# A two-layer hybrid encoder on one core: an eighth up group in seven products, early pairs split by ScalarE and DMA, and the last gate's units in program order

## The chip, the cores and the metric

The kernel runs on one core of a Trainium2 chip. Time is microseconds (us) of device time of one execution. The engines are TensorE (PE), VectorE (DVE), ScalarE (ACT), GpSimd (POOL) and SyncE (SP); SP issues the plain loads, POOL the transfers that add to what stands at their target.

## The reference

Two layers run over x of 512 tokens by 1024 channels, in float32. What matters here is cut out of the reference:

```python
for l in range(DEPTH):                       # DEPTH = 2
    h = _rmsnorm(x, g_mix[l])
    proj = h @ w_in[l]                       # gates of 4 branches, and each branch's own inputs
    ...
    y_a = _conformer_conv(a_in, ...)         # GLU, depthwise conv of width 31, LayerNorm, swish
    ...
    branch = jnp.einsum('bsnc,ncd->bsnd', ys, w_branch[l])
    gates = jax.nn.sigmoid(gate_pre.reshape(bsz, seq, N_BRANCH, D_MODEL) + gate_b[l])
    mixed = jnp.sum(gates * branch, axis=2)
    x = x + mixed @ w_out[l]
    x = x + _conv_ffn(_rmsnorm(x, g_ffn[l]), w_up[l], ffn_conv_w[l], ffn_conv_b[l], w_down[l])

def _conv_ffn(h, w_up, conv_w, conv_b, w_down):
    u = _depthwise_conv(h @ w_up, conv_w, conv_b)          # 1024 -> 2 x 2816, conv width 3
    gate, up = jnp.split(u, 2, axis=-1)
    return (jax.nn.silu(gate) * up) @ w_down
```

## The kernel before

Everything is held with channels on the partitions and the 512 tokens along the row. A float32 operand is split into a high part that TensorE takes in one pass and a low part, the rest; one product is then three matmuls: high by high, high by low, low by high. Both the weights and the activations are split so. A weight unit (128 partitions by 1024) is loaded by SP into `w_raw`; ACT copies it into `w_hi` (L269, or L1277 for units of a seven-product group), and DVE subtracts to make `w_lo` (L271, L1278). `w_raw` has two buffers, `w_hi` and `w_lo` three each, and units are made two ahead.

**Whole units and seven products.** A whole unit multiplies one weight unit by the full 512 tokens, in 24 matmuls of 512 columns (`block`, L290 to L292). Four of them make one group of the up projection (two gate blocks and two up blocks). For some groups, `SEVEN`, the group is instead treated as a 2 by 2 block product and worked out with seven smaller products rather than eight: seven units of 24 matmuls with 256 columns each (`seven`, L1130), named A11, A12, A22, S1, S2, S3 and S4. The activations' sums and differences (`form` tiles) are made once a layer. The weights' sums grow in place: POOL issues a transfer that adds another quarter of the weight matrix to a tile already used (`grow`, L1259, target `chain` or `w_raw`). Copies of partial results (`sv`, L1142, by ACT) and sums (DVE) put the seven products together.

**The last gate.** Each layer's four branches have a gate. The gate of branch `ORDER[3]`, the conv branch, runs last and as two such groups, `ga` and `gb`, 14 units in all (`last_gate`, `gate_unit`, L936). `GATE_STEPS` gives the order of the units in the program. Meanwhile a generator, `conv`, does the conv branch in steps: at each `tick` after half a unit it takes one. It transposes the conv's result (L471), makes the LayerNorm's mean and spread, normalises into `cv` tiles (L487), waits two ticks, and transposes back (L496). After unit 12 and unit 14 four branch products each follow (`branch`), and then the output projection, whose operand is `mh`.

Instructions go to the engines in an order that a scheduler chooses at build time: it takes the program's order as priority and moves an instruction back when what it needs (a PSUM bank, a buffer) is not yet free by its reckoning. Two helpers bend it: `after_mm` ties an instruction behind the last matmul in the order without a wait, and `first()` raises priority.

**The up projection.** `up_steps` makes the list of steps: whole groups 0 and 1, then the seven-product groups, whose units are interleaved with those of the next group, then the rest whole; the first two whole units after them are `held` between the last seven-product units. Each finished block is multiplied by `RB` into `U` (L1216), then goes through the width-3 convolution (`conv_part`, L1171 to L1173), and Silu (`fth`), and the product of gate and up is `f`, two blocks to a tile.

**Pairs and the down projection.** The down projection is a seven-product one too, over 11 pairs of `f` blocks, and needs each pair's sums (`sum`) and the high and low parts of all of them: `split_pair` makes them, with high copies by ACT (L1354) and low subtractions by DVE (L1355). The first six pairs are split during the up projection: after blocks 15 to 20, `EARLY`. The rest are split one at a time in the down projection's loop. `pair_tags` says into which old buffers the parts go.

```python
EARLY = (15, 16, 17, 18, 19, 20)
...
        if i in EARLY:
            self.split_pair(self.F, EARLY.index(i), self.got)
```

Of the kernel before, what the change touches and what calls it, by code (L numbers as in the profile page):

```python
# [3 lines left out]

# [2 lines left out]

# [23 lines left out]

CHUNK = 4

SEVEN = (2, 3, 4, 5, 6, 7)


def up_steps():
# [17 lines left out]
              ('gb', 'A22'), ('ga', 'S2'), ('ga', 'S1'), ('gb', 'S2'), ('gb', 'S1'), ('ga', 'S4'), ('gb', 'S4')]  # L57
MIX = (0, 1, 4, 5, 2, 3, 6, 7)

EARLY = (15, 16, 17, 18, 19, 20)  # L60
EPS = 1e-6
BIG = 1e30
EB = 4
# [167 lines left out]
class Trunk:  # L231
# [214 lines left out]
    def conv(self):  # L446
# [36 lines left out]
        for h in range(2):  # L483
# [3 lines left out]
                v.tensor_scalar(un[:, b * 256:(b + 1) * 256], pss[h][:, b * 256:(b + 1) * 256], mv[:, tb, 0:1],  # L487
                                r[:, tb:tb + 1], ALU.subtract, ALU.mult)
            uns.append(un)
        for _ in range(2):  # L490
            yield
        yh, yl = self.y_tiles()
        for j in range(2):
# [428 lines left out]
    def gate_unit(self, g, n):  # L922

        b = g, {'S3': 'B', 'A22': 'B', 'A12': 'C'}.get(n, 'A')
        start = n in ('S3', 'A11', 'A12')
        if start:
            self.banks[b] = self.mm() if n == 'A12' else self.aux()
        ps = self.banks[b]
        hi, lo = self.unit()
        for e in range(2):  # L930
            o = ps[:, e * 256:(e + 1) * 256]
            for j in range(4):
                s = slice((2 * j + e) * P, (2 * j + e + 1) * P)
                xh, xl = self.gate_x(n, j)
                for i, (w, x) in enumerate(((hi, xh), (hi, xl), (lo, xh))):
                    self.last_mm = self.nc.tensor.matmul(o, lhsT=w[:, s], rhs=x, start=start and not (e or j or i),  # L936
                                                         stop=j == 3 and i == 2, skip_group_check=True)
            self.tick()
        self.gate_done(g, n, ps)

# [222 lines left out]
    def conv_part(self, i, s):  # L1163

        nc = self.nc
        v = nc.vector
        c = i + s * NF
        u = self.U[s][:, i % 2]
        y = self.fp.tile([P, S], F32, name=f"cy{s}", tag=f"cy{s}", bufs=2)
        w = lambda t: self.par('ffn_conv_w', c * 3 + t)  # L1170
        nc.scalar.activation(y, u[:, 1:513], AF.Identity, scale=w(1), bias=self.par('ffn_conv_b', c))  # L1171
        v.scalar_tensor_tensor(y, u[:, 0:512], w(0), y, ALU.mult, ALU.add)
        v.scalar_tensor_tensor(y, u[:, 2:514], w(2), y, ALU.mult, ALU.add)  # L1173

        if s == 0:
            si = self.fp.tile([P, S], F32, name="fth", tag="fth", bufs=2)
            nc.scalar.activation(si, y, AF.Silu)
            self.silus[i] = si
            return
        if self.last and i % 2 == 1 and i // 2 < KT:  # L1180
            self.turn_res(i // 2)
        if i % 2 == 0:
            self.fpair = self.fp.tile([P, 1024], F32, name="f", tag=f"fp{i // 2}", bufs=1)
        fl = self.fpair[:, i % 2 * S:(i % 2 + 1) * S]
        v.tensor_tensor(fl, y, self.silus.pop(i), ALU.mult)
        self.F.append(fl)
        if i in EARLY:
            self.split_pair(self.F, EARLY.index(i), self.got)

    def ffn(self, l, last):  # L1190
        nc = self.nc
# [2 lines left out]
        for i in range(2):  # L1194
# [2 lines left out]
            nc.gpsimd.memset(u[:, :, 513:514], 0.0)  # L1197
            self.U.append(u)
        self.F, self.got, self.silus, self.sevens, self.last = [], {}, {}, {}, last
        self.seven_forms()  # L1200
        held = {}
        self.pace = 0.0
        for kind, a, b in UP_STEPS:
            if kind == 'seven':
                self.seven(a, b)
                continue
            if kind == 'free':
                ps = held.pop((a, b))
            else:
                ps = self.mm()  # L1210
                self.block(ps)
                self.tick()
            if kind == 'held':
                held[a, b] = ps
            else:
                v.tensor_tensor(self.U[b][:, a % 2, 1:513], ps, self.RB, ALU.mult)  # L1216
                self.conv_part(a, b)
        for g in self.slow:
            for _ in g:
# [93 lines left out]
    def pair_tags(self, j):  # L1313

        x = [f"x{n}{d}" for d in range(KT) for n in 'hl']
        late = [(f"lt{n // 2}", n % 2) for n in range(10)]
        hi = [f"fh{2 * j}", f"fh{2 * j + 1}"] if j < len(EARLY) else x[2 * (j - len(EARLY)):][:2]
        lo = ["lo", "lo"] if j == 0 else [(f"fp{j - 1}", 0), (f"fp{j - 1}", 1)]  # L1320
        a = (["e0", "e1"], ["e2", "e3"], ["e4", "e5"], late[0:2], late[2:4], late[4:6],
             ["xr", "xr"], ["xn", "xn"], ["cy0", "cy0"], ["cy1", "cy1"], x[10:12])[j]
        s4 = (late[6:8], late[8:10], ["e6", "e7"], x[12:14], x[14:16], ["t3", "t2"])[j // 2]
        return hi + lo + a + s4

    def conv_tile(self, tag):
# [3 lines left out]
    def split_pair(self, F, j, got):  # L1330
# [2 lines left out]
        v = nc.vector  # L1333
        fi, fk = F[2 * j:2 * j + 2]

        def tile(t):
            if isinstance(t, tuple):
                t, n = t
                if n == 0:
                    self.halves[t] = self.fp.tile([P, 1024], F32R, name=f"p{t}", tag=t, bufs=1)  # L1340
                return self.halves[t][:, n * S:(n + 1) * S]
            pool = self.xpool if t[:2] in ("xh", "xl") else self.fp
            return pool.tile([P, S], F32R, name=f"p{t}", tag=t, bufs=2 if t in ("lo", "xr", "xn", "cy0", "cy1") else 1)
# [353 lines left out]
```

## Time and profile before

| what | value |
|---|---|
| median of three runs | 1544.81 us (1544.36 to 1545.08) |
| the profiled execution | 1543.59 us |
| its span, first to last instruction | 1541.8 us |
| matmuls on PE | 8274 |
| up projection, layer 0 | 439.3 to 664.0 us |
| up projection, layer 1 | 1206.1 to 1433 us |
| last gate, layer 0 / layer 1 | from 333.2 / from 1099.7 us |

The median and the profiled execution are about 1.2 us apart, and the span leaves out what lies before the first and after the last instruction. In a timeline row come the start, the duration (both us), the engine, the line and operation, output and input by the program's names, the shape, a count, and in brackets the idle time before it with what ended it. A matmul's duration is longer than the distance to the next, because matmuls overlap: the pace is read from the starts. `<-DVE w_lo L1278` says that DVE's instruction on line 1278 ended the idle time.

### The profile page before, as it was taken

The page shows a single profiled execution, that of the slowest core. Times are in us where ns is not written, and L with a number is a line of the kernel's source. Part 1 is how long each engine was busy: PE and PEld are TensorE (multiplying, and loading weights), DVE is VectorE, ACT ScalarE, POOL GpSimd, SP SyncE. Part 2 cuts the span into 40 slices and gives each one's busy share as a digit, 9 for nine tenths or more (in the row PEclk, how much of TensorE's full clock was granted, in tenths as well). Part 3 has the DMA queues.
Part 4 walks back from the last instruction along what each step waited for, and adds up shares of the span by engine and source line. Part 5 has one row for each costly group of instructions (what it writes and reads, how often), then busy time and mean ns, then how long its engine had stood idle before and what let it go on. Part 6 is the DMA issues. An engine that isn't in the chain of part 4 may idle for free.

```text
span 1541.8 us, 22905 instructions
## 1 busy us (share of the span) xinstructions
PE 1528.9 (99%) x8274; PEld 1322.0 (86%) x8274; DVE 1308.0 (85%) x2210; ACT 942.8 (61%) x1580; POOL 187.7 (12%) x288
## 2 busy tenths in 40 slices
PE   9999999999999999999999999999999999999999
PEld 8888888889889999888888888888898899988887
DVE  6689988797789999996576899887986899999974
ACT  6677777356456665564548687673564566655643
POOL 0123002321001110000002130023200011100000
PEclk9999999999999999999999999999999999999999
DMA  7789586856656886366568795867566589852674
GB/s 236 227 229 203 164 181 152 181 151 148 208 168 141 178 182 162 96 205 203 180 185 255 203 202 174 171 161 182 146 150 215 171 173 230 182 155 96 191 229 161
DMA packets 117153, 278.58 MB, mean 181 GB/s; under 512 B 27440, under 2 KB 29360, under 8 KB 117040
## 3 DMA queue, kind: packets, MB, share of 16 engines
q1 hardware_dynamic: 87088, 187.98, 38.2%
q0 software_dynamic: 29664, 88.62, 30.5%
q8 instruction: 65, 1.06, 0.3%
q10 hardware_dynamic: 288, 0.52, 0.1%
q14 instruction: 48, 0.39, 0.1%
HBM read 259.25 MB, written 58.72 MB: 206 GB/s over the span
## 4 chain that ended last, share of the span: by engine, by line
PE 85%; DVE 8%; ACT 3%; issue 2%; DMA 2%; POOL 0%; ACTq 0%; DVEq 0%; POOLq 0%
PE mm L291 14%; PE mm L290 14%; PE mm L292 14%; PE aux L1130 11%; PE aux L936 3%; PE aux L1376 3%; PE aux L1378 3%; PE aux L1377 3%; PE mm L520 2%; PE mm L521 2%; PE mm L522 2%; PE mm L1376 2%; PE mm L1378 2%; PE mm L1377 2%; PE mm L1130 2%
## 5 line engine op out<-in xcount | busy, mean ns | idle before, releaser
L269 ACT ACTIVATE w_hi<-w_raw 128x1024 fp32r<-128x1024 f32 (+1 forms) x241 | 251.1, 1043 | 232.5 <-PE mm L291 83.3
L271 DVE TENSOR_TENSOR w_lo<-w_raw,w_hi 128x1024 fp32r<-128x1024 f32 (+1 forms) x241 | 290.5, 1207 | 72.8 <-ACT w_hi L269 71.3
L290 PE MATMUL mm<-xh,w_hi 128*128 128x512 f32 x768 | 300.2, 391 | 0.0
L291 PE MATMUL mm<-xl,w_hi 128*128 128x512 f32 x768 | 299.5, 390 | 0.0
L292 PE MATMUL mm<-xh,w_lo 128*128 128x512 f32 x768 | 299.3, 390 | 0.0
L292 PEld LDWEIGHTS mm<-xh,w_lo 128*128 128x128 f32 x768 | 144.2, 188 | 30.6
L290 PEld LDWEIGHTS mm<-xh,w_hi 128*128 128x128 f32 x768 | 144.3, 188 | 29.0
L291 PEld LDWEIGHTS mm<-xl,w_hi 128*128 128x128 f32 x768 | 144.3, 188 | 28.3
L1130 PE MATMUL aux<-form,w_hi 128*128 128x256 f32 x768 | 140.2, 283 | 1.4 <-ACT sv L1142 1.4
L1130 PEld LDWEIGHTS aux<-form,w_hi 128*128 128x128 f32 x768 | 120.0, 192 | 2.5 <-ACT sv L1142 2.2
L1130 PE MATMUL aux<-form,w_lo 128*128 128x256 f32 x384 | 108.7, 283 | 0.0
L1277 ACT ACTIVATE w_hi<-chain 128x1024 fp32r<-128x1024 f32 x64 | 67.6, 1057 | 53.7 <-DMA chain<-W 11.5
L457 DVE SCALAR_TENSOR_TENSOR cv<-cv,prm 128x512 f32<-128x512 f32 x120 | 94.6, 788 | 0.7
L1278 DVE TENSOR_TENSOR w_lo<-chain,w_hi 128x1024 fp32r<-128x1024 f32 x64 | 77.9, 1219 | 17.0 <-ACT w_hi L1277 16.7
L1171 ACT ACTIVATE cy<-U,prm 128x512 f32<-128x512 f32 x88 | 68.4, 808 | 32.2 <-DVE U L1216 21.0
L520 PE MATMUL mm<-w_hi,xh 128*128 128x512 f32 x192 | 76.4, 398 | 0.3 <-DVE V L648 0.3
L1277 ACT ACTIVATE w_hi<-w_raw 128x1024 fp32r<-128x1024 f32 x48 | 50.6, 1053 | 42.4 <-PE aux L1130 21.1
L521 PE MATMUL mm<-w_lo,xh 128*128 128x512 f32 x192 | 74.9, 390 | 0.0
L522 PE MATMUL mm<-w_hi,xl 128*128 128x512 f32 x192 | 74.8, 390 | 0.0
L1259 POOL DMA_DIRECT2D chain<-W x48 | 42.1, 876 | 260.4 <-DVE w_lo L1278 233.1
L1130 PEld LDWEIGHTS aux<-form,w_lo 128*128 128x128 f32 x384 | 73.7, 192 | 0.0
L777 ACT ACTIVATE e<-e,rl 128x256 f32<-128x256 f32 (+2 forms) x96 | 57.3, 597 | 21.8 <-DVE rl L776 21.5
(376 smaller groups left out, 3837.7 us busy)
## 6 DMA issues: line engine op xcount, KB each, us to landing
w_raw<-W SPq DMA_DIRECT2D x191, 512.0 KB, 4.1
sums<-W POOLq DMA_DIRECT2D x24, 1024.0 KB, 11.5
chain<-W POOLq DMA_DIRECT2D x48, 512.0 KB, 5.7
w_raw<-W SPq DMA_DIRECT2D x66, 256.0 KB, 3.7
w_raw<-sums SPq DMA_DIRECT2D x44, 256.0 KB, 3.8
w_raw<-sums SPq DMA_DIRECT2D x22, 512.0 KB, 4.3
sums<-W POOLq DMA_DIRECT2D x12, 768.0 KB, 10.7
sums<-sums POOLq DMA_DIRECT2D x8, 1024.0 KB, 7.2
```

Of the source, the lines that this page charges most:

```text
L269: w = nc.scalar.activation(hi[:, s], raw[:, s], AF.Copy)
L271: nc.vector.tensor_tensor(lo[:, s], raw[:, s], hi[:, s].bitcast(F32), ALU.subtract)
L290: mm(ps, lhsT=wh, rhs=xh, start=start, stop=False)
L291: mm(ps, lhsT=wh, rhs=xl, start=False, stop=False)
L292: self.last_mm = mm(ps, lhsT=wl, rhs=xh, start=False, stop=stop)
L457: self.after_mm(v.scalar_tensor_tensor(acc, u[:, t:t + S], w(t), acc, ALU.mult, ALU.add))
L520: mm(pss[b], lhsT=self.Xh[k][:, t], rhs=hi[:, s], start=k == 0, stop=False)
L521: mm(pss[b], lhsT=self.Xh[k][:, t], rhs=lo[:, s], start=False, stop=False)
L522: self.last_mm = mm(pss[b], lhsT=self.Xl[k][:, t], rhs=hi[:, s], start=False, stop=k == KT - 1)
L1130: self.last_mm = nc.tensor.matmul(o, lhsT=w[:, s], rhs=x, start=start and not (e or j or i), stop=j == 3 and i == 2, skip_group_check=True)
L1277: nc.scalar.activation(hi, raw, AF.Copy)
L1278: nc.vector.tensor_tensor(lo, raw, hi.bitcast(F32), ALU.subtract)
```

## The change

`SEVEN` is extended by group 8, so the up projection has seven such groups, 2 to 8, and whole groups 0, 1, 9 and 10. The first six pairs are split by a new function, `early_pair`, at other places: `(i, s)` names the block and whether it is after the gate part (0) or the product (1). ACT copies the pair's high part and the negated high part, and a transfer on POOL's queue adds `f` to the latter, which makes the low part, with no DVE work; the low part of pair j from 2 on is written where pair j-2's `f` was. The sums stay with DVE. In the gate, the first matmul of each unit is tied behind the last one before, so the units stay in the order of `GATE_STEPS`, and the conv branch waits ten ticks, not two, before it transposes back. The last blocks' evacuation into `U` is issued with `first()`.

```diff
-SEVEN = (2, 3, 4, 5, 6, 7)
+SEVEN = (2, 3, 4, 5, 6, 7, 8)
...
-EARLY = (15, 16, 17, 18, 19, 20)
+EARLY = ((17, 1), (19, 0), (19, 1), (20, 0), (20, 1), (21, 0))
...
-        for _ in range(2):
+        for _ in range(10):
             yield
         yh, yl = self.y_tiles()
...
-                    self.last_mm = self.nc.tensor.matmul(o, lhsT=w[:, s], rhs=x, start=start and not (e or j or i),
-                                                         stop=j == 3 and i == 2, skip_group_check=True)
+                    p = self.nc.tensor.matmul(o, lhsT=w[:, s], rhs=x, start=start and not (e or j or i),
+                                              stop=j == 3 and i == 2, skip_group_check=True)
+                    if not (e or j or i):
+                        self.after_mm(p)
+                    self.last_mm = p
...
+            if (i, 0) in EARLY:
+                self.early_pair(EARLY.index((i, 0)))
...
-        if i in EARLY:
-            self.split_pair(self.F, EARLY.index(i), self.got)
+        if (i, 1) in EARLY:
+            self.early_pair(EARLY.index((i, 1)))
+
+    def early_pair(self, j):
+
+        nc = self.nc
+        v = nc.vector
+        f = self.fpairs[j]
+        tags = self.pair_tags(j)
+        hi = self.fp.tile([P, 1024], F32R, name="pfh", tag=f"fh{j}", bufs=1)
+        low = self.fp.tile([P, 1024], F32R, name="plo", tag=f"fp{j - 2}" if j > 1 else f"lo{j}", bufs=1)
+        ah, al = (self.pair_tile(t) for t in tags[4:6])
+        if j % 2 == 0:
+            self.got['b'] = [self.pair_tile(t) for t in tags[6:]]
+        bh, bl = (t[:, j % 2 * 256:j % 2 * 256 + 256] for t in self.got['b'])
+        a = self.fp.tile([P, S], F32, name="sum", tag="xr", bufs=2)
+        q = lambda n: f[:, n * 256:(n + 1) * 256]
+        v.tensor_tensor(a[:, :256], q(1), q(3), ALU.subtract)
+        v.tensor_tensor(q(1), q(0), q(1), ALU.subtract)
+        nc.scalar.activation(hi, f, AF.Copy)
+        nc.scalar.activation(low, hi.bitcast(F32), AF.Copy, scale=-1.0)
+        nc.gpsimd.dma_start(low, f, accum_op=ALU.add)
+        v.tensor_tensor(a[:, 256:], a[:, :256], q(0), ALU.subtract)
+        b = self.fp.tile([P, S], F32, name="sum", tag="xr", bufs=2)[:, :256]
+        v.tensor_tensor(b, q(2), a[:, 256:], ALU.add)
+        nc.scalar.activation(ah, a, AF.Copy)
+        v.tensor_tensor(al, a, ah.bitcast(F32), ALU.subtract)
+        nc.scalar.activation(bh, b, AF.Copy)
+        v.tensor_tensor(bl, b, bh.bitcast(F32), ALU.subtract)
...
-                v.tensor_tensor(self.U[b][:, a % 2, 1:513], ps, self.RB, ALU.mult)
+                with self.first() if a >= NF - 2 else nullcontext():
+                    v.tensor_tensor(self.U[b][:, a % 2, 1:513], ps, self.RB, ALU.mult)
...
-        lo = ["lo", "lo"] if j == 0 else [(f"fp{j - 1}", 0), (f"fp{j - 1}", 1)]
+        lo = [(f"fp{j - 2}", 0), (f"fp{j - 2}", 1)]
```

How this moves instructions shows best on two engines. First PE at layer 0's last gate, behind the last matmuls of gb's A11 (`aux<-xh6` and so on). An operand `form` belongs to an S unit or A22, an operand `xh` to A11, A12 or S4. Before:

```order
L936 MATMUL aux_3845<-xh6_180,w_hi_3797 128x256
L936 MATMUL aux_3845<-xl6_181,w_hi_3797 128x256
L936 MATMUL aux_3845<-xh6_180,w_lo_3798 128x256
L936 MATMUL aux_3925<-form_3533,w_hi_3891 128x256
L936 MATMUL aux_3925<-form_3534,w_hi_3891 128x256
L936 MATMUL aux_3925<-form_3533,w_lo_3892 128x256
```

The same place on PE in the change:

```order
L936 MATMUL aux_3831<-xh6_180,w_hi_3797 128x256
L936 MATMUL aux_3831<-xl6_181,w_hi_3797 128x256
L936 MATMUL aux_3831<-xh6_180,w_lo_3798 128x256
L936 MATMUL mm_3864<-xh1_122,w_hi_3834 128x256
L936 MATMUL mm_3864<-xl1_123,w_hi_3834 128x256
L936 MATMUL mm_3864<-xh1_122,w_lo_3835 128x256
```

Before, ga's S3 comes here, and gb's A12 after it; now A12 follows at once, and S3 24 matmuls later. On PE at the end of that first S3 unit, 24 matmuls on, before, where `cst,cv` is a transpose back (L496):

```order
L936 MATMUL aux_3925<-form_3715,w_lo_3892 128x256
L496 MATMUL mm_3828<-cst_72,cv_3786 128x128
L496 MATMUL mm_3864<-cst_72,cv_3786 128x128
L936 MATMUL aux_3988<-form_3533,w_hi_3959 128x256
L496 MATMUL mm_3828<-cst_72,cv_3786 128x128
L496 MATMUL mm_3864<-cst_72,cv_3786 128x128
L936 MATMUL mm_3890<-xh1_122,w_hi_3848 128x256
L936 MATMUL mm_3890<-xl1_123,w_hi_3848 128x256
L496 MATMUL mm_3828<-cst_72,cv_3789 128x128
L496 MATMUL mm_3864<-cst_72,cv_3789 128x128
L936 MATMUL mm_3890<-xh1_122,w_lo_3849 128x256
```

And where the transposes back stand on PE in the change, behind the 48 matmuls of ga's S3 and A22:

```order
L936 MATMUL aux_3899<-form_3715,w_hi_3902 128x256
L936 MATMUL aux_3899<-form_3716,w_hi_3902 128x256
L936 MATMUL aux_3899<-form_3715,w_lo_3903 128x256
L496 MATMUL mm_3964<-cst_72,cv_3786 128x128 x2
L496 MATMUL mm_3964<-cst_72,cv_3789 128x128 x2
L936 MATMUL aux_3976<-form_3533,w_hi_3933 128x256
L936 MATMUL aux_3976<-form_3534,w_hi_3933 128x256
L936 MATMUL aux_3976<-form_3533,w_lo_3934 128x256
```

The eight transposes go from single pairs among the first matmuls of gb's S3 and A12 to two blocks of four, of which this is the first, with a half unit between them. The second place is ACT around the head of the down projection of layer 0, before (`pxh`, `pxr`, `pxl` are parts of pairs from 6 on, L1171 and L1177 belong to the width-3 convolution):

```order
L1171 ACTIVATE cy0_7105<-U0_4726,prm_73 128x512
L269 ACTIVATE w_hi_7207<-w_raw_7206 128x1024
L1171 ACTIVATE cy1_7144<-U1_4729,prm_73 128x512
L269 ACTIVATE w_hi_7244<-w_raw_7243 128x1024
L1177 ACTIVATE fth_7109<-cy0_7105 128x512
L269 ACTIVATE w_hi_7262<-w_raw_7261 128x1024
L269 ACTIVATE w_hi_7301<-w_raw_7300 128x1024
L1354 ACTIVATE pxh0_7168<-f_6400 128x512
L1354 ACTIVATE pxr_7171<-sum_7175 128x512
L1354 ACTIVATE pxl4_7393<-f_7054 128x512
L269 ACTIVATE w_hi_7319<-w_raw_7318 128x1024
```

The same place on ACT in the change (`pfh` is an early pair's high part, `plo` its negated copy):

```order
L269 ACTIVATE w_hi_7294<-w_raw_7293 128x1024
L1212 ACTIVATE pfh_7126<-f_5910 128x1024
L1218 ACTIVATE plt1_7128<-sum_7131 128x512
L1213 ACTIVATE plo_7127<-pfh_7126 128x1024
L269 ACTIVATE w_hi_7331<-w_raw_7330 128x1024
L1220 ACTIVATE pe6_7129<-sum_7138 128x256
L1180 ACTIVATE fth_7180<-cy0_7176 128x512
L1212 ACTIVATE pfh_7182<-f_6155 128x1024
L269 ACTIVATE w_hi_7349<-w_raw_7348 128x1024
L1213 ACTIVATE plo_7183<-pfh_7182 128x1024
L1218 ACTIVATE plt2_7184<-sum_7185 128x512
```

The early pairs' copies, 1024 wide and two to a pair, now stand between the down projection's weight copies.

More of the change, by code (lines that the diff above doesn't have):

```diff
@@ L7 @@
-from contextlib import ExitStack
+from contextlib import ExitStack, nullcontext
 from itertools import chain
@@ L1183, in conv_part @@
             self.fpair = self.fp.tile([P, 1024], F32, name="f", tag=f"fp{i // 2}", bufs=1)
+            self.fpairs.append(self.fpair)
         fl = self.fpair[:, i % 2 * S:(i % 2 + 1) * S]
@@ L1186, in conv_part, with pair_tile @@
         self.F.append(fl)
-        if i in EARLY:
-            self.split_pair(self.F, EARLY.index(i), self.got)
+        if (i, 1) in EARLY:
[25 more added lines that the diff above has]
+        v.tensor_tensor(bl, b, bh.bitcast(F32), ALU.subtract)
+        cut = lambda h, l, c: [(h[:, c + b * P:c + (b + 1) * P], l[:, c + b * P:c + (b + 1) * P]) for b in range(2)]
+        self.got[j] = {'a11': cut(hi, low, 0), 's1': cut(hi, low, 256), 'a12': cut(hi, low, 512),
+                       's4': cut(hi, low, 768), 's3': cut(ah, al, 0), 's2': cut(ah, al, 256), 'a22': cut(bh, bl, 0)}
+    def pair_tile(self, t):
+        if isinstance(t, tuple):
+            t, n = t
+            if n == 0:
+                self.halves[t] = self.fp.tile([P, 1024], F32R, name=f"p{t}", tag=t, bufs=1)
+            return self.halves[t][:, n * S:(n + 1) * S]
+        pool = self.xpool if t[:2] in ("xh", "xl") else self.fp
+        return pool.tile([P, S], F32R, name=f"p{t}", tag=t, bufs=2 if t in ("xr", "xn", "cy0", "cy1") else 1)
     def ffn(self, l, last):
@@ L1199, in ffn @@
         self.F, self.got, self.silus, self.sevens, self.last = [], {}, {}, {}, last
+        self.fpairs = []
         self.seven_forms()
@@ L1319, in pair_tags @@
         hi = [f"fh{2 * j}", f"fh{2 * j + 1}"] if j < len(EARLY) else x[2 * (j - len(EARLY)):][:2]
-        lo = ["lo", "lo"] if j == 0 else [(f"fp{j - 1}", 0), (f"fp{j - 1}", 1)]
+        lo = [(f"fp{j - 2}", 0), (f"fp{j - 2}", 1)]
         a = (["e0", "e1"], ["e2", "e3"], ["e4", "e5"], late[0:2], late[2:4], late[4:6],
              ["xr", "xr"], ["xn", "xn"], ["cy0", "cy0"], ["cy1", "cy1"], x[10:12])[j]
-        s4 = (late[6:8], late[8:10], ["e6", "e7"], x[12:14], x[14:16], ["t3", "t2"])[j // 2]
+        s4 = (late[6:8], late[8:10], ["e6", "e7"], x[12:14], x[14:16], [("fp9", 0), ("fp9", 1)])[j // 2]
         return hi + lo + a + s4
@@ L1334, in split_pair @@
         fi, fk = F[2 * j:2 * j + 2]
[L1336 to L1343, printed above, removed]
+        tile = self.pair_tile
         tags = self.pair_tags(j)
```

## The prediction

> **What bounds the kernel now.** I read the page's head first, then TensorE's waits, then the timeline of the stages that the change touches.
>
> ```profile
> span 1541.8 us, 22905 instructions
> PE 1528.9 (99%) x8274; PEld 1322.0 (86%) x8274; DVE 1308.0 (85%) x2210; ACT 942.8 (61%) x1580; POOL 187.7 (12%) x288
> PEclk9999999999999999999999999999999999999999
> PE 85%; DVE 8%; ACT 3%; issue 2%; DMA 2%; POOL 0%; ACTq 0%; DVEq 0%; POOLq 0%
> ```
>
> TensorE (PE) is busy for 99% of the span, at full clock in every slice, and 85% of the chain that ended last is PE. So an edit gains only where it takes matmul time away, or one of PE's few waits:
>
> ```profile
> engine line waited for: us in total, times, longest us
> PE aux L936 <- DVE w_lo L1278: 3.3, 4, 1.0
> PE mm L496 <- DVE cv L487: 2.0, 2, 1.0
> PE aux L1130 <- ACT sv L1142: 1.4, 2, 1.1
> ```
>
> The first two rows, 5.3 us, lie in the last gate; the third lies in layer 1's up projection. The change aims at the gate's waits and at the number of matmul columns. VectorE (DVE) at 85% is the engine to fear: it makes every w_lo that PE loads.
>
> **The gate's order.** PE's timeline in layer 0, from the stage's start over its three stalls to its end, then start and end in layer 1:
>
> ```profile
> 333.18 0.28 PE L936 MATMUL aux<-xh,w_hi 128*128 128x256 f32 x1
> ...
> 342.69 0.40 PE L936 MATMUL aux<-form,w_hi 128*128 128x256 f32 x2
> 343.84 0.38 PE L936 MATMUL aux<-form,w_lo 128*128 128x256 f32 x1 [0.76 <-DVE w_lo L1278]
> ...
> 346.46 0.28 PE L936 MATMUL aux<-form,w_lo 128*128 128x256 f32 x1
> 347.73 0.44 PE L496 MATMUL mm<-cst,cv 128*128 128x128 f32 x2 [1.00 <-DVE cv L487]
> ...
> 364.58 0.39 PE L936 MATMUL aux<-form,w_lo 128*128 128x256 f32 x1 [0.76 <-DVE w_lo L1278]
> ...
> 389.87 0.39 PE L290 MATMUL mm<-mh,w_hi 128*128 128x512 f32 x1
> ...
> 1099.68 0.28 PE L936 MATMUL aux<-xh,w_hi 128*128 128x256 f32 x1
> ...
> 1156.61 0.39 PE L290 MATMUL mm<-mh,w_hi 128*128 128x512 f32 x1
> ```
>
> To price the stage without stalls I need the pace of both matmul shapes. A whole unit and a unit of a seven-product group, 24 matmuls each, stand side by side in the up projection:
>
> ```profile
> 461.07 0.39 PE L290 MATMUL mm<-xh,w_hi 128*128 128x512 f32 x1
> ...
> 466.51 0.28 PE L1130 MATMUL aux<-xh,w_hi 128*128 128x256 f32 x1
> ...
> 469.38 0.40 PE L290 MATMUL mm<-xh,w_hi 128*128 128x512 f32 x1
> ```
>
> 512 columns: 5.44 us, 226.7 ns each. 256 columns: 2.87 us, 119.6 ns each. The gate stage holds 14 units of 24 narrow matmuls (336 x 0.120 = 40.3), 8 branch products of 6 wide ones (48 x 0.2267 = 10.9) and 16 transposes at an estimated 0.1 each (1.6): 52.8 us. It lasts 389.87 - 333.18 = 56.7 in layer 0 and 1156.61 - 1099.68 = 56.9 in layer 1. So 3.9 and 4.1 us are lost, **8.0 in all**. The waits show only 5.3, since a stall costs more than its bracket: from 342.69 to 343.84 are 1.15 us for two matmuls of 0.24 together, 0.91 lost for 0.76 shown.
>
> The cause is order: PE takes ga's S3 before gb's A12, though DVE makes A12's w_lo first. These rows of DVE end S3's w_lo and the normalised `cv` tiles that the transposes back wait for:
>
> ```profile
> 342.57 1.22 DVE L1278 TENSOR_TENSOR w_lo<-chain,w_hi 128x1024 fp32r<-128x1024 f32 x1
> ...
> 347.13 1.45 DVE L487 TENSOR_SCALAR cv<-mm,mv,rln 128x256 f32<-128x256 f32 x3
> ...
> 349.63 0.54 DVE L487 TENSOR_SCALAR cv<-mm,mv,rln 128x256 f32<-128x256 f32 x1
> ```
>
> In the new order A12 (24 x 0.12 = 2.9 us) runs first, so S3 starts at 345.6 and needs its w_lo, finished at 343.8, with 1.8 us to spare. The transposes back stand 72 matmuls behind A12's first, not 24 behind S3's: 342.69 + 72 x 0.12 = 351.3 against a `cv` finished at 350.2, 1.1 us to spare. For the third stall I placed the finished weights of before against the new order and found about 1 us, with some 0.6 for the branch weights. The lower bound of the gain is zero (the margins are of about the size of the stalls), the upper 8.0. I take **7.0**, near the upper, because each of the three stalls has a margin by these rows; 1.0 stays for the tight ones. The ticks that the transposes now wait (10 instead of 2) cost nothing by themselves, as the branch products that need them come 5 units later.
>
> **The eighth group.** Group 8 of each layer goes from four whole units (4 x 5.44 = 21.76 us) to seven narrow ones (7 x 2.88 = 20.16). POOL's issues show that a seven-product group really keeps this pace, one per group:
>
> ```profile
> 521.05 0.88 POOL L1259 DMA_DIRECT2D w_raw<-W  x1 [5.23 <-DVE w_lo L1278]
> ...
> 541.20 0.88 POOL L1259 DMA_DIRECT2D w_raw<-W  x1 [5.25 <-DVE w_lo L1278]
> ...
> 561.37 0.87 POOL L1259 DMA_DIRECT2D w_raw<-W  x1 [5.25 <-DVE w_lo L1278]
> ```
>
> 20.15 and 20.17 us. So it saves 1.6 a layer, **3.2 us** in all. A rule weighs differently here: the Trainium skill, "TensorE: Matmul & The Clock Gate", section "Wait — 56ns, not 53.3ns?", has a warm matmul start every N / 2.4 GHz plus about 2.5 ns. By it a layer would save 96 x 215.8 - 168 x 109.2 ns = 2.4 us, 4.7 in all, and the sum would come out 1.5 lower; this trace's 226.7 and 119.6 ns disagree, and they decide.
>
> What the group adds elsewhere: three more w_hi, w_lo, three more copies and three more 512-wide sums. Its weights need four more growing transfers of 512 KB a layer on POOL's queue, with DMA at 0.42 in the window from 600 below; I count them as hidden. What pays for the group is the early pairs' split. The rows by form (600 to 720 us):
>
> ```profile
> L271 DVE TENSOR_TENSOR w_lo<-w_raw,w_hi 128x1024 fp32r<-128x1024 f32 x33 | 40.2, 1218 | 9.5 <-ACT w_hi L269 9.4
> L1355 DVE TENSOR_TENSOR pfp<-f,pfh 128x512 fp32r<-128x512 f32 x10 | 6.7, 682 | 0.0
> L1354 ACT ACTIVATE pfh<-f 128x512 fp32r<-128x512 f32 x4 | 2.5, 620 | 0.2 <-DVE f L1358 0.2
> L269 ACT ACTIVATE w_hi<-w_raw 128x1024 fp32r<-128x1024 f32 x33 | 35.0, 1059 | 29.2 <-PE mm L1378 11.2 <-PE aux L1378 6.5 <-PE mm L291 4.6
> ```
>
> DVE gets 3 x 1.22 + 3 x 0.68 = 5.7 us more a layer, and loses two 512-wide subtractions in each of six pairs, 12 x 0.68 = 8.2: 2.5 less. ScalarE (ACT) gets 3 x 1.06 + 3 x 0.62 for the group, and 2 x 1.06 in place of 2 x 0.62 per pair: 5.0 + 5.3 = 10.3 us more. Whether that is hidden, the windows say (PE, PEld, DVE, ACT in order):
>
> ```profile
> 600.00:610.00 10.00, 10.00 (x62) 8.98 (x61) 10.00 (x15) 4.90 (x7) 0.00 (x0) 1.00 0.42 136
> ...
> 664.00:674.00 10.00, 10.00 (x46) 8.29 (x45) 9.99 (x16) 6.84 (x9) 0.00 (x0) 1.00 0.54 166
> 674.00:684.00 10.00, 10.00 (x46) 8.29 (x45) 10.00 (x18) 6.84 (x10) 0.00 (x0) 1.00 0.90 292
> ```
>
> DVE is full from 600 on and PE waits for nothing, so DVE's queue holds slack work; ACT has 3 to 5 us free in 10. The added 10.3 fit in the up's last 64 us. The risk is the head of the down projection, where pairs 3 to 5 are now split and PE's margin is small:
>
> ```profile
> 668.63 1.22 DVE L271 TENSOR_TENSOR w_lo<-w_raw,w_hi 128x1024 fp32r<-128x1024 f32 x1
> ...
> 672.37 0.39 PE L1377 MATMUL aux<-w_lo,pfh 128*128 128x512 f32 x1
> ```
>
> That w_lo was finished 2.5 us before its use. ACT's extra there is 3 x 0.88 = 2.6 us a layer, between nothing (its free 3.2 us in each ten) and all of it, 5.2 us in both. I take **0.4** for the whole tail, since the ACT rows show it waiting for PE to free a weight buffer (11.2 us), work that can shift. The last `U` evacuations, now issued first, only change DVE's order: each is one row of 0.68 us like those above, and what they overtake is the slack work; if they overtook a w_lo, that would be inside the 5.2.
>
> The third change of that stage is the accumulating transfer that makes each low part. The next row of this kind is the one that grows a weight tile, and the slowest is the 1 MB load:
>
> ```profile
> chain<-W POOLq DMA_DIRECT2D x48, 512.0 KB, 5.7
> sums<-W POOLq DMA_DIRECT2D x24, 1024.0 KB, 11.5
> ```
>
> Pair j's low part is written where pair j-2's f was, so ACT waits there until that transfer has landed. In the new order the ACT instructions between sum to at least 11.6 us by these durations; 5.7 is far below, 11.5 just at it. I take nothing.
>
> **Sum.** 1543.6 (the profiled execution; its span is 1541.8) - 7.0 - 3.2 + 0.4 = 1533.8. The median of the runs shown is 1.2 above the profiled one: **1535.0**.
>
> **Rivals.**
> - ACT's 5.2 us in the head of the down projection are not hidden: 1535.0 + 5.2 = 1540.2. For it, full DVE and a margin of 2.5 us; against it, ACT's free time. Part of it is likelier than all.
> - More than forecast: the last 1.0 us of the gate goes too, and the two waits on `sv` in layer 1 (1.4 shown, some 1.9 with what a stall loses besides), as ACT no longer stands behind a split: 1535.0 - 1.0 - 1.9 = 1532.1. A fixed part of 2 x 119.6 - 226.7 = 12.5 ns per narrow matmul, were it absent in the new group, would give 7 x 24 x 12.5 = 2.1 a layer, less the whole units' 1.2: 1533.2. No row speaks for it, and it shares this case's chance.
> - The gate's stalls only move: S3's w_lo or the branch weights come later in the new order as well. Then 7.0 stay and the time is 1542.0.
> - **Slower:** the accumulating transfers are late. If one takes 17 us from issue to landing (5.7 + 11.5, one behind another), ACT stands 17 - 11.6 = 5.4 us at pair 4, which is 2.9 beyond PE's margin, and 5.4 again at pair 5, with the margin gone: 8.3 a layer, 16.6 in both, 1551.6. Pairs 2 and 3 come earlier, where PE's units leave more room. It turns the sign from 16 us on. For it, a DMA share of 0.90 at 674 to 684; against it, the queue, which is idle there before (POOL 0.00 in the windows). The Trainium skill speaks for it: "SBUF — State Buffer", section "SBUF: two separate sides", says that a busy DVE can keep GpSimd from writing descriptors, five times as long in its example. By that the sum would go to this rival; the 0.87 to 0.88 us of POOL's issues above, beside a DVE at 85%, show no such stretch.
>
> **How the numbers follow.** Chances: forecast (1533 to 1537) 0.55, ACT's cost 0.20, more 0.10, stalls move 0.08, late transfers 0.07. The range from 1531.7 to 1541.5 leaves out the last two and little else. A measurement of this kernel can tell 0.2%, 3.1 us, from no change: faster is below 1541.7, which the first three cases are (0.85); the moved stalls are the same (0.08); slower 0.07.
>
> **What would show it.** Right: no wait on `w_lo` or `cv` at the gate, the stage at 53 to 54 us; group 8 in 20.2; no PE wait in the first 20 us of the down. Wrong: a wait of PE on L271's w_lo there, with ACT behind a low part or a 1024-wide copy; an accumulating transfer of over 11.6 us; or a `w_lo` wait at another unit of the gate.

## The result and the profile after

The changed kernel takes 1551.8 us (median of six runs, 1550.6 to 1555.4) against 1544.6 us for the kernel before on the same chips. The ratio is 1.0053, 95% interval 1.0042 to 1.0063: it is **slower by about 8 us** (7.2 by the two medians), where 9.8 us faster was forecast. The profiled execution took 1551.46 us.

First the page's head after the change (span; busy time of the engines; the clock that PE was granted, by slices), then PE's waits:

```profile
span 1549.7 us, 23233 instructions
PE 1530.7 (99%) x8418; PEld 1329.3 (86%) x8418; DVE 1304.4 (84%) x2198; ACT 959.7 (62%) x1592; POOL 205.3 (13%) x308
...
PEclk9999999999999999999999999999999999999999
...
PE aux L936 <- ACT sv L952: 8.6, 7, 1.5
PE aux L1416 <- DVE w_lo L271: 3.3, 1, 3.3
```

The two kinds of wait that stood at the gate before (on `w_lo` and on `cv`) are gone, as forecast. In their place stand seven waits on `sv`, ScalarE's copy of a PSUM bank (the memory into which TensorE adds up its results), at the same stage, and one of 3.3 us in the down projection. Part of the loss stands in PE's busy time, which is 1.8 us longer with fewer matmul columns: some matmuls ran at half clock, as the windows further down show. The slices of the clock, 39 us each, are too coarse to show it.

PE's starts cut both executions into stages. The lengths, in us:

| stage | before | after | difference |
|---|---|---|---|
| up to the first gate | 333.18 | 333.90 | +0.7 |
| gate, layer 0 | 56.69 | 58.18 | +1.5 |
| output and up projection, layer 0 | 274.11 | 272.70 | -1.4 |
| from there to the gate of layer 1 | 435.70 | 435.75 | 0.0 |
| gate, layer 1 | 56.93 | 58.45 | +1.5 |
| output and up projection, layer 1 | 276.48 | 275.40 | -1.1 |
| down projection, layer 1 | 104.49 | 110.95 | +6.5 |

The cuts of the down projection run to PE's last matmul there. The differences sum to +7.7; the spans differ by 7.9. So the second layer's down projection and the two gates have lost 9.5 us, and the up projections have gained 2.5.

**The gate.** PE's timeline after the change, layer 0 with its three waits, and the stage's ends in layer 1:

```profile
333.90 0.28 PE L936 MATMUL aux<-xh,w_hi 128*128 128x256 f32 x1
...
349.05 0.28 PE L936 MATMUL aux<-form,w_lo 128*128 128x256 f32 x1
350.85 0.50 PE L936 MATMUL aux<-form,w_hi 128*128 128x256 f32 x2 [1.52 <-ACT sv L952]
...
358.89 0.50 PE L936 MATMUL aux<-form,w_hi 128*128 128x256 f32 x2 [1.18 <-ACT sv L952]
...
366.42 0.50 PE L936 MATMUL aux<-form,w_hi 128*128 128x256 f32 x2 [1.51 <-ACT sv L952]
...
392.08 0.39 PE L290 MATMUL mm<-mh,w_hi 128*128 128x512 f32 x1
...
1100.53 0.28 PE L936 MATMUL aux<-xh,w_hi 128*128 128x256 f32 x1
...
1158.98 0.39 PE L290 MATMUL mm<-mh,w_hi 128*128 128x512 f32 x1
```

And ScalarE in front of the first of them:

```profile
349.25 1.06 ACT L1324 ACTIVATE w_hi<-w_raw 128x1024 fp32r<-128x1024 f32 x1 [1.77 <-PE aux L936]
350.21 0.58 ACT L952 ACTIVATE sv<-aux 128x512 f32<-128x512 f32 x1
```

Six of the seven waits, three in each layer, stand where one unit ends and another begins on the same bank: ga's S3 and A22, gb's S3 and A22, ga's S2 and S1. The seventh is 0.2 us long. S3's result must be copied out before A22 adds to the bank. In the order of `GATE_STEPS` these two follow each other at once, so PE waits for the whole copy (0.58) and for nearly all of the weight copy of 1.06 that ScalarE takes first.

**The down projection of layer 1.** DVE, POOL and PE at its head:

```profile
1438.75 0.87 POOL L1214 DMA_DIRECT2D plo<-f  x1 [5.60 <-ACT plo L1213]
...
1449.79 0.69 DVE L1394 TENSOR_TENSOR pfp<-f,pxl 128x512 fp32r<-128x512 f32 x1 [5.38 <-DMA plo<-f]
1450.40 1.22 DVE L271 TENSOR_TENSOR w_lo<-w_raw,w_hi 128x1024 fp32r<-128x1024 f32 x1
...
1447.98 0.39 PE L1415 MATMUL aux<-w_hi,pfh 128*128 128x512 f32 x1
1451.68 0.80 PE L1416 MATMUL aux<-w_lo,pfh 128*128 128x512 f32 x1 [3.31 <-DVE w_lo L271]
```

The accumulating transfer of pair 4 is issued at 1438.75 and lands 11.0 us later. VectorE's low subtraction of pair 6 writes into the buffer that this transfer reads, and waits 5.4 us. The weight's low part stands behind it in VectorE's queue, so PE waits 3.3 us. The same stretch by windows (PE, PEld, DVE, ACT and POOL busy, then the granted clock, the DMA share and GB/s):

```profile
1434.40:1448.20 13.80, 13.80 (x62) 11.24 (x60) 9.94 (x19) 13.67 (x20) 1.74 (x2) 1.00 0.95 239
1448.20:1451.70 3.50, 0.19 (x2) 0.03 (x1) 1.91 (x3) 1.06 (x1) 0.00 (x0) 0.89 0.80 194
1451.70:1457.60 5.90, 5.90 (x14) 4.66 (x15) 5.90 (x9) 0.82 (x1) 0.00 (x0) 0.50 0.65 174
1457.60:1460.00 2.40, 2.40 (x11) 1.94 (x11) 2.40 (x6) 1.07 (x3) 0.00 (x0) 0.97 0.93 303
```

From the last start before the wait to the first behind it are 3.7 us (1447.98 to 1451.68), 3.5 more than the pace. After the wait PE's clock is 0.50 for 5.9 us: 14 matmuls start 0.43 us apart instead of 0.23, another 2.8 us. Wait and slow clock together cost 6.3 of the stage's 6.5 us. In layer 0 the same transfer (issued at 668.76) held VectorE for only 0.74 us and PE did not wait:

```profile
675.16 0.69 DVE L1394 TENSOR_TENSOR pfp<-f,pxl 128x512 fp32r<-128x512 f32 x1 [0.74 <-DMA plo<-f]
```

### The profile page after: what moved, and what is told of

Its sections match the earlier page's. It is cut to its first block, busy times and chain, and to the rows that moved or that the text cites. A ratio compares the mean times of both kernels' runs of the same rounds, so it can differ in the third digit from the quotient of the medians.

```text
span 1549.7 us, 23233 instructions
## 1 busy us (share of the span) xinstructions
PE 1530.7 (99%) x8418; PEld 1329.3 (86%) x8418; DVE 1304.4 (84%) x2198; ACT 959.7 (62%) x1592; POOL 205.3 (13%) x308
## 4 chain that ended last, share of the span: by engine, by line
PE 82%; DVE 10%; ACT 4%; DMA 2%; issue 2%; DVEq 0%; ACTq 0%
PE mm L291 12%; PE mm L290 12%; PE mm L292 12%; PE aux L1133 10%; PE aux L936 4%; PE aux L1416 3%; PE aux L1417 3%; PE aux L1415 2%; PE mm L520 2%; PE mm L522 2%; PE mm L521 2%; PE mm L1416 2%; PE mm L1415 2%; PE mm L1417 2%; PE aux L813 2%
## 5 line engine op out<-in xcount | busy, mean ns | idle before, releaser
L271 DVE TENSOR_TENSOR w_lo<-w_raw,w_hi 128x1024 fp32r<-128x1024 f32 (+1 forms) x233 | 280.7, 1206 | 67.3 <-ACT w_hi L269 66.0
L290 PE MATMUL mm<-xh,w_hi 128*128 128x512 f32 x704 | 275.3, 391 | 0.0
L291 PE MATMUL mm<-xl,w_hi 128*128 128x512 f32 x704 | 274.6, 390 | 0.0
L292 PE MATMUL mm<-xh,w_lo 128*128 128x512 f32 x704 | 274.4, 390 | 0.0
L1133 PE MATMUL aux<-form,w_hi 128*128 128x256 f32 x896 | 163.6, 283 | 0.2
L292 PEld LDWEIGHTS mm<-xh,w_lo 128*128 128x128 f32 x704 | 132.2, 188 | 28.2
L290 PEld LDWEIGHTS mm<-xh,w_hi 128*128 128x128 f32 x704 | 132.2, 188 | 26.5
L1133 PEld LDWEIGHTS aux<-form,w_hi 128*128 128x128 f32 x896 | 140.0, 192 | 1.3 <-ACT sv L1145 1.0
L1133 PE MATMUL aux<-form,w_lo 128*128 128x256 f32 x448 | 127.0, 283 | 0.0
L1324 ACT ACTIVATE w_hi<-chain 128x1024 fp32r<-128x1024 f32 x72 | 76.0, 1057 | 53.4 <-PE mm L1133 14.9
L1133 PEld LDWEIGHTS aux<-form,w_lo 128*128 128x128 f32 x448 | 86.0, 192 | 0.4 <-DVE w_lo L1325 0.4
L1325 DVE TENSOR_TENSOR w_lo<-w_raw,w_hi 128x1024 fp32r<-128x1024 f32 x54 | 65.8, 1219 | 11.1 <-ACT w_hi L1324 10.7
```

What stands on the lines that cost most here:

```text
L271: nc.vector.tensor_tensor(lo[:, s], raw[:, s], hi[:, s].bitcast(F32), ALU.subtract)
L290: mm(ps, lhsT=wh, rhs=xh, start=start, stop=False)
L291: mm(ps, lhsT=wh, rhs=xl, start=False, stop=False)
L292: self.last_mm = mm(ps, lhsT=wl, rhs=xh, start=False, stop=stop)
L1133: self.last_mm = nc.tensor.matmul(o, lhsT=w[:, s], rhs=x, start=start and not (e or j or i), stop=j == 3 and i == 2, skip_group_check=True)
L1324: nc.scalar.activation(hi, raw, AF.Copy)
```

## The experiments

All were timed in five rounds beside the kernel before. As chips and rounds differ a little, ratios to the kernel before are compared. By their intervals, a difference between two of the ratios is known to about 0.0015, 2 to 3 us:

| run | median us | before us | ratio (95%) |
|---|---|---|---|
| the change | 1551.8 | 1544.6 | 1.0053 (1.0042 to 1.0063) |
| e1 gate as before | 1546.9 | 1543.4 | 1.0025 (1.0015 to 1.0036) |
| e2 gate interleaved | 1542.4 | 1543.4 | 0.9991 (0.9982 to 1.0000) |
| e3 pair 6 later | 1544.7 | 1543.4 | 1.0009 (1.0000 to 1.0018) |
| e4 lows 4 and 5 by VectorE | 1545.3 | 1543.4 | 1.0014 (1.0005 to 1.0023) |
| e5 e2 and e3 | 1539.1 | 1544.2 | 0.9965 (0.9954 to 0.9977) |
| e6 e5 without group 8 | 1538.6 | 1544.2 | 0.9965 (0.9952 to 0.9977) |
| e7 e5, all lows by VectorE | 1537.8 | 1544.2 | 0.9958 (0.9944 to 0.9971) |
| e8 e5 with two ticks | 1551.7 | 1544.2 | 1.0046 (1.0033 to 1.0058) |
| e9 before, gate interleaved | 1539.5 | 1543.8 | 0.9973 (0.9963 to 0.9984) |
| e10 e2, all lows by VectorE | 1537.1 | 1543.8 | 0.9963 (0.9950 to 0.9975) |
| e11 e10 without group 8 | 1538.7 | 1543.8 | 0.9965 (0.9951 to 0.9978) |
| e12 residual loads later | 1546.0 | 1543.8 | 1.0014 (1.0006 to 1.0023) |

**e1, the gate's two edits taken back.**

```diff
-        for _ in range(10):
+        for _ in range(2):
...
-                    if not (e or j or i):
-                        self.after_mm(p)
```

> The changed kernel with its two edits to the last gate taken back: units no longer tied to program order, two ticks before the transposes back. Theory (program order costs the gate 1.5 us a layer against before, since A22 follows S3 and S1 follows S2 at once and must wait until ScalarE has copied the same bank): the gate stage is 56.7 and 56.9 us again as before, the waits of PE on sv at the gate are gone and those on w_lo and cv are back, and the time is about 3 us below the changed kernel's 1551.8, near 1548.8. Rival (the gate is neutral and the loss lies elsewhere): within 1 us of the changed kernel.

The gate stages came out at 56.7 us in both layers, and the waits on `w_lo` and `cv` were back:

```profile
PE aux L936 <- DVE w_lo L1325: 3.0, 4, 0.8
PE mm L496 <- DVE cv L487: 2.0, 2, 1.0
```

The ratio fell by 0.0028, 4.3 us, somewhat more than the 3 expected from the stages alone but within the intervals. So the change's gate cost time.

**e2, another program order.** Only the table changes:

```diff
-... ('ga', 'S3'), ('ga', 'A22'), ('gb', 'S3'), ('gb', 'A22'), ('ga', 'S2'), ('ga', 'S1'), ('gb', 'S2'), ('gb', 'S1'), ...
+... ('ga', 'S3'), ('gb', 'S3'), ('ga', 'A22'), ('gb', 'A22'), ('ga', 'S2'), ('gb', 'S2'), ('ga', 'S1'), ('gb', 'S1'), ...
```

> The changed kernel with another program order in the last gate: S3 of ga, S3 of gb, A22 of ga, A22 of gb, S2 of ga, S2 of gb, S1 of ga, S1 of gb, so that a unit of the other half lies between two units on one bank. Theory: a unit of 2.9 us covers the copy, all seven waits on sv go, none on w_lo comes back, the gate stage falls from 58.2 and 58.5 to 53 to 53.5 us, and the time by about 10 us from 1551.8 to about 1541.5. Rival (with the banks free the next late thing is a w_lo or the transposes, as before): the stage stays above 55.5 us and the time above 1546.

PE's starts at the two ends of the stage in both layers, and its waits:

```profile
333.12 0.28 PE L936 MATMUL aux<-xh,w_hi 128*128 128x256 f32 x1
...
386.29 0.39 PE L290 MATMUL mm<-mh,w_hi 128*128 128x512 f32 x1
...
1096.45 0.28 PE L936 MATMUL aux<-xh,w_hi 128*128 128x256 f32 x1
...
1150.43 0.39 PE L290 MATMUL mm<-mh,w_hi 128*128 128x512 f32 x1
```

```profile
PE aux L1416 <- DVE w_lo L271: 3.8, 1, 3.8
...
PE aux L936 <- ACT sv L952: 0.8, 1, 0.8
PE mm L291 <- DVE ml L1018: 0.6, 2, 0.3
```

The stages are 53.2 and 54.0 us. Six of the seven waits on `sv` are gone, none on `w_lo` came back at the gate, and the run is 9.6 us faster than the change by the ratios. The gate's term was possible; this order gets 6.5 us of it in the two stages. The wait in the down projection is untouched, so the two losses are separate.

**e3, pairs 6 to 10 split later.**

```diff
-            if todo:
+            if j > 2 and todo:
                 self.split_pair(F, todo.pop(0), got)
...
-            v.tensor_tensor(l, x, h.bitcast(F32), ALU.subtract)
+            self.after_mm(v.tensor_tensor(l, x, h.bitcast(F32), ALU.subtract))
```

> The changed kernel with pairs 6 to 10 split three pairs later in the down projection, so that VectorE's first subtraction into the buffer of pair 4's f stands behind three more weight subtractions; every transfer stays. Theory (the buffer: VectorE waits 5.4 us in its queue for pair 4's accumulating transfer, and the weights behind it are late): that wait and PE's 3.3 us with the slow clock behind it in layer 1 are gone, about 6.3 us less than 1551.8, near 1545.5. Rival (contention: weight loads land 9 to 10 us after issue there, so ScalarE and PE are late anyway): PE still waits 1.5 us or more at that place and the time is above 1548.5.

The ratio fell by 0.0044, 6.8 us. The wait of PE and the slow clock were gone: this is VectorE's only kind of wait left in 1430 to 1460 us:

```profile
DVE w_lo L271 <- ACT w_hi L269: 1.8, 3, 1.4
```

Every transfer was still there, and the one of pair 4 in layer 1 took 10.7 us, against 11.0 in the change. So the place of the waiting instruction in VectorE's queue, not the transfers' load on the weights, made PE wait.

**e4, the low parts of pairs 4 and 5 by VectorE.**

```diff
+        if j in (4, 5):
+            v.tensor_tensor(low, f, hi.bitcast(F32), ALU.subtract)
+        else:
             nc.scalar.activation(low, hi.bitcast(F32), AF.Copy, scale=-1.0)
             nc.gpsimd.dma_start(low, f, accum_op=ALU.add)
```

> The changed kernel with the low parts of pairs 4 and 5 made by VectorE's subtraction instead of ScalarE's copy and the accumulating transfer: 1 MB less of transfer, 2 us less of ScalarE and 2.4 us more of VectorE at the head of each down projection. Both theories expect the wait in layer 1 to go, near 1545.5; if VectorE is the bound there (my forecast's worry), the added 2.4 us a layer shows as PE waits on w_lo in both layers, above 1548.

The ratio fell by 0.0039, 6.0 us, and PE had no wait on `w_lo` in either down projection. Two more subtractions a layer on a full VectorE, in place of two transfers, cost nothing that the time shows.

**e5 to e8** build on e2 and e3 together; e6 takes group 8 out, e7 has VectorE make all early low parts, e8 goes back to two ticks:

```diff
-SEVEN = (2, 3, 4, 5, 6, 7, 8)
+SEVEN = (2, 3, 4, 5, 6, 7)
...
-        nc.scalar.activation(low, hi.bitcast(F32), AF.Copy, scale=-1.0)
-        nc.gpsimd.dma_start(low, f, accum_op=ALU.add)
+        v.tensor_tensor(low, f, hi.bitcast(F32), ALU.subtract)
...
-        for _ in range(10):
+        for _ in range(2):
```

> The interleaved gate order and the later split of pairs 6 to 10 together. If the two losses are separate, their gains add: 9.2 us and 6.1 us below the changed kernel, about 1536 where the kernel before has 1543.4, ratio 0.995; gate stages of 53 to 54 us and no wait of PE above 1 us in the down projection. If both gains come from the same slack (weights made in time), the sum is below 12 us and the time above 1539.

> As the run before it, but group 8 whole again (six seven-product groups). Theory of the forecast (narrow matmuls save 1.6 us a layer, and what the group adds to VectorE and ScalarE is hidden): 3.2 us slower than with group 8, about 1539. Rival (what the group adds is paid in late weights): within 1 us of it. By the matmul page's N / 2.4 GHz plus 2.5 ns it would be 4.7 us slower.

> As e5, but all six early pairs' low parts by VectorE's subtraction: no accumulating transfer of that kind, 12 us less of ScalarE and 14 us more of VectorE over both layers. Theory (VectorE is the engine to fear at the end of the up projection, so the transfer is what lets group 8 in): new waits of PE on w_lo or sv at the end of the up and the head of the down, 2 us or more over both layers. Rival (VectorE's queue has that much slack): within 0.7 us of e5.

> As e5, but two ticks rather than ten before the conv branch transposes back. In this order the transposes stand ahead of and among the first matmuls of gb's A12, about 5 us of PE time earlier than the normalised tiles are finished in the trace of before. Theory (ten ticks are part of the gain): PE waits 4 to 6 us for cv in each layer, the gate stage is 57 to 60 us, and after waits this long the clock is low for some microseconds as in the changed kernel's down projection; 8 to 14 us slower than e5. Rival: the tiles come in time, as VectorE follows, and the stage is 54 to 55 us, within 2 us of e5.

e5 gained 13.6 us by the ratios, where 15.3 was expected; that lies between its two theories, and nearer to the sum of both gains. Its gate stages are 53.7 us each, and its longest wait in a down projection is 0.5 us, as expected. New waits took some of the gain, most of them in layer 1. These are PE's waits in e5:

```profile
PE aux L1133 <- ACT sv L1145: 1.3, 1, 1.3
...
PE aux L936 <- ACT sv L952: 0.9, 2, 0.5
PE mm L291 <- DVE ml L1018: 0.6, 2, 0.3
PE aux L1133 <- DVE w_lo L1325: 0.5, 1, 0.5
PE mm L1416 <- DVE w_lo L271: 0.5, 1, 0.5
```

e6 has the same ratio as e5: there, **no gain of group 8 shows**. In the profiled execution of each, the output and up projections of layer 0 together took 273.1 us with it and 274.7 without, close to the 1.6 of the forecast; in layer 1 they took 277.1 and 276.5, and the down projection 105.8 and 104.5. So the gain of layer 0 was given back in layer 1, in part at waits such as the first, fourth and fifth above (2.2 us; e6 has one of 0.5 us of these kinds).

e7 was not slower than e5 but 0.0007 faster, inside the intervals. ScalarE's copies and the accumulating transfers, which were to relieve VectorE, gain nothing that can be measured here.

e8 was 0.0081 slower than e5, 12.5 us. The gate stages took 60.5 and 60.3 us, with one wait in each layer:

```profile
348.86 0.47 PE L496 MATMUL mm<-cst,cv 128*128 128x128 f32 x1 [4.90 <-DVE cv L487]
...
349.00:351.00 2.00, 2.00 (x10) 1.84 (x11) 1.16 (x3) 0.00 (x0) 0.00 (x0) 0.50 0.97 178
```

The ten ticks, which I had called free, are a condition of the gain: without them the transposes are placed early, and PE stands still until VectorE has normalised. The window behind shows the low clock again.

**e9, the gate alone.** The kernel before with the order of e2 and ten ticks, nothing else:

> The kernel before with nothing changed but the last gate: the interleaved order of e2 and ten ticks before the transposes back. Theory (the gate's term of my forecast was right in size, and only the order that the change chose takes it back): gate stages of 53 to 54 us in both layers, 3.5 and 3 us less than before, and 6 to 6.5 us faster than the kernel before, ratio 0.996. Rival (part of the loss only moves behind the stage, to the output projection): below 4 us.

The stages were 53.4 and 53.7 us, 6.5 less in both together, and the time fell by 0.0027, 4.2 us (2.5 to 5.7 by the interval); the profiled execution fell by 5.4. So most but not all of the stage's gain arrived. In the profiled execution 0.4 us are lost before the first gate, and the output and up projections are 0.7 us longer in layer 0 and some 0.2 in layer 1; two waits on `ml` at their start (0.6 us, absent before) account for most of that. The median run is another 1.3 us slower than the profiled one, and no profile shows where.

**e10 and e11, without the transfers, with and without group 8.**

> The changed kernel with the interleaved gate order and all early low parts by VectorE, pairs 6 to 10 split where the change splits them. Without accumulating transfers nothing holds the buffer of pair 4's f, so the later split should not be needed: within 1 us of 1537.8 where the kernel before has 1544.2. Rival (the head of the down projection is also short of VectorE time): a wait on w_lo there, 2 us or more slower than e7.

> As e10, but group 8 whole. In e5 and e6 the group's gain was given back by waits in layer 1. If the accumulating transfers' share of the DMA queues caused that, the group saves 2.5 to 3.2 us here, so this run is that much slower than e10; if it is the group's own weights and copies (ScalarE's and the transfers that grow them), this run is within 1 us of e10.

e10 was as fast as e7, so without the transfers the later split isn't needed. By the medians e11 was 1.7 us slower than e10, by the ratios 0.3, with intervals that overlap nearly whole. In the profiled executions the output and up projections are shorter with group 8, by 1.5 us in layer 0 and 0.7 in layer 1. So the group may be worth some 2 us in this setting or nothing, and what gave its gain back in e5 stays open. In e10's profiled execution, its slowest with 1542.2 us against 1536.5 to 1537.3 in the four others, PE waited 5.2 us for `sv` at the gates, 2.2 in layer 0 and 3.0 in layer 1. In layer 1:

```profile
1133.72 1.06 ACT L269 ACTIVATE w_hi<-w_raw 128x1024 fp32r<-128x1024 f32 x1 [5.66 <-DMA w_raw<-W]
1134.68 0.58 ACT L952 ACTIVATE sv<-aux 128x512 f32<-128x512 f32 x1
...
1135.31 0.52 PE L936 MATMUL aux<-form,w_hi 128*128 128x256 f32 x2 [2.96 <-ACT sv L952]
```

A weight load was late there (ScalarE waited 5.7 us for it), and the copy of the bank stands behind its `w_hi` on ScalarE. That is the weak place of the interleaved order: e2, e5, e9 and e11 have waits on `sv` there too, of up to 1.0 us.

By their medians e10 and e7 are the fastest versions of the study, 0.4% below the kernel before and about 0.9% below the change; both keep group 8, both have the interleaved gate, and neither has the accumulating transfers of the early pairs.

**e12, why layer 1 and not layer 0.** In layer 1 two loads of the residual (`U<-resT`, 256 KB each) are issued just ahead of pair 4's transfer:

```profile
1438.28 0.99 SPq L1436 DMA_DIRECT2D U<-resT  x2
```

The edit issues four such loads at the seventh pair of the down projection instead:

```diff
+            if j == 6:
+                us = [self.conv_tile(f"U{i}") for i in range(2)]
+                xt = {(b, 0): us[b // 2][:, b % 2, :S] for b in range(NB)}
+                if last:
+                    for b, h in ((2, 0), (3, 0), (0, 0), (1, 0)):
+                        self.after_mm(nc.sync.dma_start(xt[b, h], self.resT[b * P:(b + 1) * P, h * S:(h + 1) * S]))
```

> The changed kernel with four loads of the residual (256 KB each) issued at the seventh pair of the down projection; in the changed kernel two of them stand right before pair 4's accumulating transfer in layer 1, and layer 0 has none there. Theory (these two loads make that transfer 11.0 us long in layer 1 against 6.4 in layer 0): it lands in 7 to 8.5 us, PE's wait of 3.3 us and the slow clock behind it go, about 5 to 6 us less than the changed kernel, ratio to before near 1.0015. Rival (weight loads and the two other accumulating transfers fill the DMA anyway): 10 us or more to land, the wait stays above 2.5 us, ratio 1.005.

Issue, VectorE's wait and PE's wait in e12:

```profile
1439.22 0.87 POOL L1214 DMA_DIRECT2D plo<-f  x1 [5.60 <-ACT plo L1213]
...
1447.08 0.70 DVE L1394 TENSOR_TENSOR pfp<-f,pxl 128x512 fp32r<-128x512 f32 x1 [2.19 <-DMA plo<-f]
...
1448.96 0.50 PE L1416 MATMUL aux<-w_lo,pfh 128*128 128x512 f32 x1 [0.46 <-DVE w_lo L271]
```

The transfer landed 7.9 us after issue, PE waited 0.5 us at full clock, and the ratio fell by 0.0039, 6.0 us. So these loads made most of the difference between the layers: 7.9 us is left against the change's 6.4 in layer 0, and in e12 itself the same transfer took 7.4 in layer 0.

## Why the prediction was wrong

**The gate, -7.0 forecast, +3.0 measured.** The failed step is to take 7.0, with zero as the lower bound, because each of the three stalls has a margin: I checked the new order against when weights and `cv` tiles are finished, and against nothing else. Those margins held: neither the change nor e2 waits for `w_lo` or `cv` at the gate. But program order also brings units together that share a bank, and I did not ask what A22 needs besides its weights. The kernel shows it: `gate_unit` gives S3 and A22 of one half the same bank (`'B'`), and `gate_done` copies that bank out in between. Before, the scheduler's order had put gb's S3 and A12 behind ga's S3, and PE had no wait on `sv` at the gate; so the disorder that cost 8.0 us also hid this copy. For another order the size was nearly right in the stages: e2 has 53.2 and 54.0 us, 107.2 in both, against twice the 52.8 counted plus 1.0 kept, 106.6. In the time, e9 shows 4.2 us of the 7.0.

**The whole tail, +0.4 forecast, +6.5 measured in layer 1.** The failed step is "I take nothing" for the accumulating transfers. The mechanism was among the rivals, with the wrong victim. I let ScalarE wait, at pair j's low part for the transfer of pair j-2, and found 11.6 us between. But the same line of `pair_tags` sends pair 6's low part, which VectorE makes, into the buffer of pair 4's `f`. From issue to that instruction are only 5.7 us, and the median of the nearest row was 5.7 too: no margin. Hence a transfer of 16 us was not needed for a loss; 11.0 was enough for 6.3 us of it. ScalarE waited for no accumulating transfer there. So the sign that I had set out, a wait of PE on L271's `w_lo` in the first 20 us, came, but with VectorE behind the transfer. That a busy VectorE holds up POOL does not show either: POOL's issues took 0.87 us here too. Alone this loss does not turn the sign, since e2, which keeps it, is not slower than the kernel before; it took both failed steps. The rival got 0.07, and that its 1551.6 us stands beside the measured 1551.8 is chance: it had 8.3 us in each layer by ScalarE and a gate gain of 7.0, where the runs show 6.5 us in one layer by VectorE and a gate loss of 3.0. Nor did I have the slow clock behind a long wait in any term; it is 2.8 of the 6.3 us.

**Group 8, -3.2 forecast, -2.5 measured.** The up and output projections gave 1.4 and 1.1 us. In layer 0 the step was right. In layer 1 waits took a part: counted by PE's starts against its pace, that stage lost 2.6 us before and 3.2 in the change, where many delays of 0.1 to 0.4 us replace the two waits on `sv`. e5 and e6 show that even this gain can be given back whole. The group saved what the trace's pace gives (1.5 us, e5 against e6 in layer 0; forecast 1.6), not the estimate of 2.4 that follows from the Trainium skill's "TensorE: Matmul & The Clock Gate", section "Wait — 56ns, not 53.3ns?".

**The engine to fear.** I named VectorE, and ScalarE's extra work as the likeliest cost. e4 and e7 give VectorE 2 and 6 more wide subtractions a layer, in place of as many ScalarE copies and transfers, without a loss. It had slack where its windows showed it full. The edit that issues the last `U` evacuations first was not run by itself.

The remaining +0.7 us lies before the first gate, in code that the change leaves alone. It is there by 55 us: in that execution PE's matmuls still start 0.43 us apart, half the pace, at 5.2 to 6.9 us from its start, where in the execution before they start 0.23 to 0.34 us apart from 5 us on.

## What to carry to other kernels

When units are put in a fixed order, list for each what it reuses (bank, buffer) as well as what it reads: two units on one accumulator need a third between them that is longer than the copy out, with whatever stands ahead of that copy on its engine. When a transfer takes over an engine's work, follow its source buffer to the next writer, on every engine, and ask what stands behind that writer in its queue. Before a scheduler's disorder is replaced by an order, ask which waits the disorder hid.

## What the runs showed of the hardware

A wait of PE of about 3 us costs more than itself. After waits of 1.2 to 2.2 us the clock stayed at 1.00; after 2.96 (e10), 3.3 (the change), 3.6 (e1), 3.8 (e2) and 4.9 us (e8) it fell to 0.50. It stayed there for 3.4 us in e10 and e1 and for 6.8 us in the change, e2 and both layers of e8; the time is counted from the drop, which in the change lies 0.8 us before the wait's end. So the length of the wait alone does not give the price, and the 2.8 us above are not a fixed cost. Two windows of e10's profile, behind its waits of 2.2 us (layer 0) and 2.96 us (layer 1):

```profile
371.00:373.00 2.00, 2.00 (x16) 1.87 (x15) 2.00 (x4) 1.62 (x3) 0.00 (x0) 1.00 0.80 254
...
1137.00:1139.00 2.00, 2.00 (x11) 2.00 (x11) 2.00 (x3) 0.91 (x3) 0.00 (x0) 0.50 0.85 254
```

The Trainium skill, "TensorE: Matmul & The Clock Gate", section "What's actually happening", puts the drop to half clock after an idle window of about 3.4 us that runs freely. The half clock agrees, and 3.4 and 6.8 us are about one and two such windows; here a shown wait of 2.96 us was already enough.

An accumulating transfer of 512 KB within SBUF took 6.4 us in one layer and 11.0 in the other, with two 256 KB loads just ahead of it as most of the difference (7.9 without them). This repeats: in the change, e1, e2, e3, e5 and e8 it took 6.1 to 7.0 us in layer 0 and 10.7 to 11.3 in layer 1. For a transfer that something waits for, the median of its kind is no bound.
